# An encoder's feed-forward: every gate/up chunk by seven products, two of them run ahead

## The chip, the core and the metric

The kernel runs on one NeuronCore of a Trainium2 chip. TensorE multiplies, ScalarE and VectorE do elementwise work, GpSimd (POOL) a few small things, and DMA queues issued from SyncE (SP), ScalarE and POOL move data. The metric is the device time of one execution in microseconds (us); the time of a kernel is the median of its runs.

## The reference

Two layers over 512 tokens of width 1024, all in float32. Each layer has an attention and a convolution part with an output projection, and then a gated feed-forward:

```python
h = rms_norm(x, pre_ffn_norm[l])
g, u = jnp.split(jnp.einsum('bsd,df->bsf', h, w_gate_up[l]), 2, axis=-1)
f = jnp.einsum('bsf,fd->bsd', jax.nn.silu(g) * u, w_down[l])
x = x + rms_norm(f, post_ffn_norm[l])
```

FFN is 2816, that is 22 chunks of 128 hidden channels. Nothing else of the reference is touched by the change.

## The kernel before

**Precision.** A float32 product is made of three matmuls in a reduced format: each operand is split in a high part (a cast on ScalarE, `wh`, `big`) and a low part (a subtraction on VectorE, `wl`, `big`), and hi·hi, hi·lo and lo·hi are summed in PSUM. Weights come as `raw` tiles of 512 KB (three buffers), two for a gate/up chunk, and are split before use. `hT` are the normed tokens, turned by TensorE so that width lies on the partitions, split, in two halves of the width (g) with 512 tokens each; `raw` tiles of the same name in `out_proj` hold the turned tokens unsplit.

**An ordinary chunk** (`pair_part`) multiplies 8 slices of the width, gate and up, three matmuls each: 48 matmuls of 512 columns.

**A chunk by seven products** (`seven`) is Winograd's form of Strassen's method. The 2x2 block product of weights (width halves by gate/up) and tokens (width halves by token halves) takes seven products of 12 matmuls of 256 columns. `prepare` forms the weight differences t1 to t4 on VectorE and splits them; `make_sums` forms the four token sums once per layer, from all tokens. Products b11 and b21 give the gate for the first 256 tokens and need no sums and only the first half of the tokens; t4 gives the gate of the second half; t1, t2, t3 and b22 use the sums. Two banks y, used in turn, and banks x and q collect them.

**Order.** Chunks 0 to 3 are ordinary; 0 and 1 are done first for tokens 0 to 255 while token tiles 2 and 3 are still being normed in `out_proj`, and `turning` lets TensorE turn tile 2 inside chunk 0 and tile 3 inside chunk 1. The second halves of 0 and 1, then 2 and 3, cover `make_sums` and the first `prepare`. Chunks 4 to 21 go by seven products. TensorE's and SP's orders are those of the program text (`manual_schedule`); ScalarE's and VectorE's rows are ordered by the scheduler from the same text. Each engine has a list of its own and waits on semaphores for the others. Then the down projection splits each chunk's activation (`split`) and multiplies by the down weights.

**In `seven`, what stands between a product and the next one into the same bank** (lines 818 to 836):

```python
product(x, ops["b11"], hA[0:2], 0, 0, True)
nc.scalar.copy(y[:, :HS], x[:, :HS])
product(q, ops["t1"], sums, 1, 1, True)
product(y, ops["t2"], sums, 0, 0, False)
product(x, ops["b21"], hA, 1, 0, False)
nc.scalar.activation(gate[:, :HS], x[:, :HS], AF.Silu)
```

In ScalarE's list a row ACT_TABLE_LOAD stands where the program goes from the Ln and Exp of the norms (`rsqrt_mean`) to Silu, and where it goes back; in each layer of the kernel before that is once ahead of the first Silu and once, by `log_table`, behind the last.

## Time and profile before

| | |
|---|---|
| time, median of 3 runs | 1183.0 us (1182.74 to 1183.59) |
| the profiled execution | 1181.35 us, of it 1179.6 us span |
| TensorE (PE) busy | 1161.3 us, 98% |
| VectorE (DVE) busy | 788.5 us, 67% |
| ScalarE (ACT) busy | 628.4 us, 53% |
| granted TensorE clock | 0.998 |
| weight DMAs (`raw`), 512 KB | 192, 3.7 us from issue to landing |
| ACT_TABLE_LOAD | 6, 1283 ns each |

Matmuls overlap, so the start of one to the start of the next says how fast they go, not the duration that stands in a row. In the same way rows of VectorE and ScalarE overlap their successors by about 0.1 us. In lists of instructions a row ends with the idle time before it and who ended that, in brackets. L811 is the matmul in `product`, L190 to L192 the three of `mm3`, L241 the turning, L246 the low part of the turned tokens, L234 a norm, L761 and L762 the weight splits of `prepare`.

### The profile page before, as it was taken

To read this page: it belongs to the slowest core of one execution; us is meant where nothing else is said; L and a number is where in the kernel's file an instruction comes from. 1 tells how busy PE (TensorE), PEld (TensorE's weight loads), DVE (VectorE), ACT (ScalarE), POOL (GpSimd) and SP (SyncE) were. 2 spreads that over 40 slices of the span, in tenths; PEclk is the share of its full clock that TensorE was granted. 3 is DMA by queue.
4 is the path that set the end of the run, shared out by engine and by line. 5 is a ranking of instruction groups with operands and counts; after the bars stand their busy time and mean duration, and the time that the engine had idled before them with its cause. 6 is when DMAs were issued, how large, how long until landed. Compare 5 with 4: busy or idle time off the path is not lost.

```text
span 1179.6 us, 17833 instructions
## 1 busy us (share of the span) xinstructions
PE 1161.3 (98%) x7000; PEld 1018.9 (86%) x7000; DVE 788.5 (67%) x1330; ACT 628.4 (53%) x1217; POOL 33.8 (3%) x55
## 2 busy tenths in 40 slices
PE   9999999989999999999999999999999999999997
PEld 7777778888999999888877777788899999998886
DVE  4798655786888888432557986458868888883323
ACT  7577544663565557331445775437636555582311
POOL 5000001000000000000000000100000000000000
PEclk9999999999999999999999999999999999999999
DMA  8221123123333333423132211322223333333221
GB/s 320 90 72 54 55 66 112 56 98 99 107 99 103 106 107 110 158 74 114 46 117 80 72 54 57 99 95 72 79 90 103 106 108 108 108 126 123 91 72 72
DMA packets 33205, 114.38 MB, mean 97 GB/s; under 512 B 3936, under 2 KB 3936, under 8 KB 33120
## 3 DMA queue, kind: packets, MB, share of 16 engines
q1 hardware_dynamic: 32400, 112.15, 29.1%
q8 instruction: 55, 0.90, 0.3%
q10 hardware_dynamic: 720, 1.09, 0.2%
q14 instruction: 30, 0.25, 0.1%
HBM read 111.12 MB, written 2.10 MB: 96 GB/s over the span
## 4 chain that ended last, share of the span: by engine, by line
PE 92%; DVE 4%; ACT 2%; issue 1%; DMA 0%; DVEq 0%; SPq 0%
PE acc L811 18%; PE att L811 13%; PE acc L190 13%; PE acc L192 13%; PE acc L191 13%; PE att L190 4%; PE att L192 4%; PE att L191 4%; PE pv L427 3%; PE att L420 2%; PE att L403 1%; PE att L404 1%; ACT mid L232 1%; PE pv L192 1%; PE pv L190 1%
## 5 line engine op out<-in xcount | busy, mean ns | idle before, releaser
L178 DVE TENSOR_TENSOR wl<-raw,wh 128x1024 fp32r<-128x1024 f32 x120 | 146.5, 1222 | 165.5 <-ACT wh L177 164.9
L177 ACT CAST wh<-raw 128x1024 fp32r<-128x1024 f32 x120 | 125.7, 1050 | 177.7 <-PE acc L192 67.4
L811 PE MATMUL acc<-big,wh 128*128 128x256 f32 x1152 | 212.0, 283 | 0.0
L190 PE MATMUL acc<-big,wh 128*128 128x512 f32 (+1 forms) x496 | 184.8, 372 | 0.0
L191 PE MATMUL acc<-big,wh 128*128 128x512 f32 (+1 forms) x496 | 180.1, 363 | 1.1 <-DVE big L246 1.1
L192 PE MATMUL acc<-big,wl 128*128 128x512 f32 (+1 forms) x496 | 180.1, 363 | 0.0
L811 PEld LDWEIGHTS acc<-big,wh 128*128 128x128 f32 x1152 | 179.8, 192 | 0.2
L811 PE MATMUL acc<-big,wl 128*128 128x256 f32 x576 | 163.0, 283 | 0.0
L811 PE MATMUL att<-big,wh 128*128 128x256 f32 x864 | 160.4, 283 | 0.0
L811 PEld LDWEIGHTS att<-big,wh 128*128 128x128 f32 x864 | 134.7, 192 | 0.2
L811 PE MATMUL att<-big,wl 128*128 128x256 f32 x432 | 122.3, 283 | 0.0
L762 DVE TENSOR_TENSOR wl<-t,wh 128x1024 fp32r<-128x1024 f32 x72 | 88.0, 1223 | 43.0 <-ACT wh L761 43.0
L761 ACT CAST wh<-t 128x512 fp32r<-128x512 f32 x144 | 88.7, 619 | 45.9 <-PE att L811 31.7
L811 PEld LDWEIGHTS acc<-big,wl 128*128 128x128 f32 x576 | 110.6, 192 | 0.0
L192 PEld LDWEIGHTS acc<-big,wl 128*128 128x128 f32 x496 | 93.6, 189 | 15.2
L190 PE MATMUL acc<-wh,big 128*128 128x512 f32 x272 | 106.4, 391 | 0.2 <-ACT wh L524 0.2
L191 PEld LDWEIGHTS acc<-big,wh 128*128 128x128 f32 x496 | 93.8, 189 | 14.5 <-DVE big L246 1.7
L191 PE MATMUL acc<-wl,big 128*128 128x512 f32 x272 | 106.1, 390 | 0.2 <-DVE wl L525 0.2
L192 PE MATMUL acc<-wh,big 128*128 128x512 f32 x272 | 105.9, 389 | 0.0
L190 PEld LDWEIGHTS acc<-big,wh 128*128 128x128 f32 x496 | 93.7, 189 | 13.7 <-issue 0.8
L190 PE MATMUL att<-wh,big 128*128 128x512 f32 x228 | 89.4, 392 | 0.0
L761 ACT CAST wh<-raw 128x512 fp32r<-128x512 f32 x108 | 63.4, 619 | 48.5 <-PE acc L811 31.3
(212 smaller groups left out, 1942.9 us busy)
## 6 DMA issues: line engine op xcount, KB each, us to landing
raw<-in_w SPq DMA_DIRECT2D x192, 512.0 KB, 3.7
gain<-in_rows SPq DMA_DIRECT2D x7, 512.0 KB, 5.6
big<-in_xT SPq DMA_DIRECT2D x8, 256.0 KB, 5.5
raw<-in_w SPq DMA_DIRECT2D x8, 256.0 KB, 5.5
x<-in_x SPq DMA_DIRECT2D x4, 512.0 KB, 7.0
out_dram<-x SPq DMA_DIRECT2D x4, 256.0 KB, 2.1
out_dram<-x ACTq DMA_DIRECT2D x4, 256.0 KB, 2.1
mask_sb<-in_mask SPq DMA_DIRECT2D x1, 448.0 KB, 7.7
```

The source lines that it names most:

```text
L177: nc.scalar.copy(hi, raws[i])
L178: nc.vector.tensor_sub(lo, raws[i], hi.bitcast(F32))
L190: nc.tensor.matmul(o, sh, mh, start=start, stop=False)
L191: nc.tensor.matmul(o, sh, ml, start=False, stop=False)
L192: nc.tensor.matmul(o, sl, mh, start=False, stop=stop)
L232: nc.scalar.activation(h[:, c], x_sb[t][:, c], AF.Square, accum_out=ss[:, f:f + 1])
L403: nc.tensor.matmul(sc, qk[:, hd, q0:q0 + P], qk[:, 2 + hd, :], start=True, stop=False)
L420: nc.tensor.transpose(tp[:, k * P:(k + 1) * P], sm[:, k * P:(k + 1) * P], ident)
L427: nc.tensor.matmul(o[hd * 64:hd * 64 + 64, half * 256:half * 256 + 256], V[:, k, hc:hc + 64], PT[hd][:, k, :], start=k == 0, stop=k == NT - 1)
L761: nc.scalar.copy(hi[:, c:c + 512], src[:, c:c + 512])
L762: nc.vector.tensor_sub(lo[:, :n], src[:, :n], hi[:, :n].bitcast(F32))
L811: nc.tensor.matmul(o[:, :HS], sh[:, c], mh[:, k, :], start=start and k == 0 and n == 0, stop=k == 3 and n == 2, skip_group_check=True)
```

## The change

All 22 chunks go by seven products. The seven are cut in two functions. `lead(m)` does b11 and b21, into one bank x: b11's result is copied to the second half of the chunk's place in SBUF (`unsplit`), then b21 is added and Silu of the sum goes to the first half. `rest(m)` fetches b11's result from there into y and does t1, t2, t3 and b22; t4 (`last_product`) of a chunk is done inside the next chunk's `rest`. Six leads go ahead of all rests; tile 2 is turned behind lead 0 and tile 3 behind lead 4, each followed by its half of `make_sums`. The other 16 leads are spread over the 21 rests that have a next one, so six chunks have a rest alone. A lead loads the columns it needs of its weights by itself (two DMAs of 256 KB), and `rest` loads the whole 1 MB again. From lead 6 on its weights take the place of x in SBUF; x is written to DRAM by POOL's queue after the residual and read back behind the last chunk. Activations wait unsplit in free tiles of several kinds (`unsplit`), and the first four are split during the last chunk.

The diff, cut to its core (`load_rest` loads a `raw` half once; `quarter` takes a column range now):

```diff
-NDIRECT = 2
-
-SEVEN = 4
+LEAD = 6
+
+TURN_LEAD = {0: 2, 4: 3}
...
-    x_sb = [cpool.tile([P, D], F32, tag=f"x{t}", name=f"x{t}") for t in range(NT)]
+    x_sb = [sb.tile([P, D], F32, tag="x", bufs=4, name=f"x{t}") for t in range(NT)]
+    dpool = ctx.enter_context(tc.tile_pool(name="dpool", bufs=1, space=bass.MemoryType.DRAM))
+    x_away = dpool.tile([P, NT, D], F32, tag="x_away", name="x_away")
...
+    def load_lead(l, m):
+        if (l, m) in lead_raws:
+            return
+        if m < LEAD:
+            r = sb.tile([P, 1024], F32, tag="raw", bufs=RAW_AHEAD + 1, name=nm("raw"))
+        else:
+            r = sb.tile([P, D], F32, tag="x", bufs=4, name=nm("raw"))
+        lead_raws[l, m] = r
+        for k in range(2):
+            nc.sync.dma_start(r[:, k * 512:k * 512 + 512], w[l * NCHUNK + 16 + m][:, k * 1024:k * 1024 + 512])
+
+    def split_lead(l, m):
+        if (l, m) not in leads:
+            leads[l, m] = split_pair(lead_raws[l, m], 1024, ("wh", "wl") if m < LEAD else ("x", "x"))
+
+    def split_pair(src, n=1024, tags=("wh", "wl")):
+        hi, lo = (sb.tile([P, 1024], F32R, tag=t, bufs=4, name=nm(t)) for t in tags)
+        for c in range(0, n, 512):
+            nc.scalar.copy(hi[:, c:c + 512], src[:, c:c + 512])
+        nc.vector.tensor_sub(lo[:, :n], src[:, :n], hi[:, :n].bitcast(F32))
+        return [(hi[:, c:c + 512], lo[:, c:c + 512]) for c in range(0, n, 512)]
...
             hs[t] = normed(t, gffn)
+            nc.gpsimd.dma_start(x_away[:, t, :], x_sb[t])
...
+        def make_sums(j):
+
+            part = [[quarter(raw, g, f, j * P, P) for f in range(2)] for g in range(2)]
...
         def prepare(m):
...
+                load_rest(m, k)
+            (b11, b12), (b21, b22) = ((raws[i + k][:, :512], raws[i + k][:, 512:]) for k in range(2))
...
+            load_rest(m + 1, 1)
+            nc.vector.tensor_sub(t34[:, 512:], b21, t12[:, 512:])
             ops["t1"], ops["t2"] = split_pair(t12)
             yield
             ops["t3"], ops["t4"] = split_pair(t34)
             yield
+            ops["b22"], = split_pair(b22, 512)
+            yield
...
+        def lead(m):
+            x = bank("acc")
+            place = unsplit(m)
+            b11, b21 = leads[l, m]
+            product(x, b11, hT, 0, 0, True)
+            nc.scalar.copy(place[:, HS:], x[:, :HS])
+            product(x, b21, hT, 1, 0, False)
+            nc.scalar.activation(place[:, :HS], x[:, :HS], AF.Silu)
+
+        def last_product(m, y, up):
+            place = unsplit(m)
+            product(y, made.pop(m)["t4"], hT, 1, 1, False)
+            nc.scalar.activation(place[:, HS:], y[:, :HS], AF.Silu)
+            nc.vector.tensor_mul(place, up, place)
+
+        def rest(m, y, before, ahead):
...
+            nc.scalar.copy(y[:, :HS], unsplit(m)[:, HS:])
+            product(q, ops["t1"], sums, 1, 1, True)
+            nc.scalar.copy(p5, q[:, :HS])
+            next(ahead)
+            product(y, ops["t2"], sums, 0, 0, False)
+            nc.scalar.copy(up[:, :HS], y[:, :HS])
+            next(ahead)
+            if before is not None:
+                last_product(*before)
+            next(ahead)
+            product(y, ops["t3"], sums, 0, 1, False)
+            nc.scalar.copy(up[:, HS:], y[:, :HS])
+            nc.vector.tensor_add(up[:, HS:], up[:, HS:], p5)
+            product(q, ops["b22"], sums, 1, 0, False)
+            nc.vector.tensor_add(up[:, :HS], q[:, :HS], up[:, :HS])
+            next(ahead)
+            return m, y, up
...
+        for m in range(LEAD):
+            for k in range(m, min(m + 3, LEAD)):
+                load_lead(l, k)
+                split_lead(l, k)
+            if m + 3 < LEAD:
+                load_lead(l, m + 3)
+            lead(m)
+            if m in TURN_LEAD:
+                t = TURN_LEAD[m]
+                transposed(t, hs[t], hT, "att", raw)
+                make_sums(t - 2)
+            if m == LEAD - 3:
+                ahead = prepare(0)
+            if ahead is not None:
+                next(ahead)
+        next(ahead)
...
+        led = LEAD
+        load_lead(l, led)
+        before = None
+        for m in range(MT):
+            if led < MT:
+                split_lead(l, led)
+            before = rest(m, ys[m % 2], before, prepare(m + 1) if m + 1 < MT else down_splits())
+            if led < LEAD + (m + 1) * (MT - LEAD) // (MT - 1) and led < MT:
+                lead(led)
+                led += 1
+                if led < MT:
+                    load_lead(l, led)
+        last_product(*before)
+        for t in range(NT):
+            x_sb[t] = sb.tile([P, D], F32, tag="x", bufs=4, name=nm("x"))
+            nc.gpsimd.dma_start(x_sb[t], x_away[:, t, :])
```

**On TensorE, between b11 and b21.** `acc` and `att` are banks, `big` token tiles, `wh`/`wl` split weights. Before, in the first seven-product chunk, the last two matmuls of t2 and the first of b21:

```order
L811 MATMUL att_2779<-big_2575,wh_2730 128x256
L811 MATMUL att_2779<-big_2574,wl_2731 128x256
L811 MATMUL acc_2783<-big_2045,wh_2748 128x256
L811 MATMUL acc_2783<-big_2047,wh_2748 128x256
L811 MATMUL acc_2783<-big_2045,wl_2749 128x256 [waits DVE_49]
```

Now, in lead 0, the last two of b11 and the first of b21:

```order
L818 MATMUL acc_2370<-big_2049,wh_2288 128x256
L818 MATMUL acc_2370<-big_2047,wl_2289 128x256
L818 MATMUL acc_2370<-big_2048,wh_2288 128x256 [waits Activation_49]
L818 MATMUL acc_2370<-big_2050,wh_2288 128x256 [waits DVE_49]
L818 MATMUL acc_2370<-big_2048,wl_2289 128x256
```

b21 now follows b11 at once in the same bank and waits for ScalarE's copy of it (L829); t1 and t2 no longer stand between.

**On ScalarE, where the norms of the last tokens meet the first Silu.** Before, the first Silu (L722) stands behind all Ln and Exp rows (L208, L210) of `out_proj`; the turned tokens (L245, L248) come first:

```order
L248 COPY big_2049<-att_2412 128x4x128 [waits DVE_49]
L210 ACTIVATE small_2343<-small_2343 128x1 [waits Activation_49]
L245 CAST big_2044<-att_2468 128x4x128 [waits PE_49]
L245 CAST big_2045<-att_2476 128x4x128 [waits PE_49]
L248 COPY big_2048<-att_2468 128x4x128 [waits DVE_49]
L248 COPY big_2049<-att_2476 128x4x128 [waits DVE_49]
L752 CAST big_2521<-big_2049 128x4x256 [waits DVE_49]
L177 CAST wh_2558<-raw_2356 128x1024 [waits DMAHW1_49,PE_49]
L722 ACT_TABLE_LOAD
L722 ACTIVATE tmp_2550<-acc_2352 128x512 [waits PE_49]
```

Now the Silu of lead 0 (L831) stands among the Ln (L253) and Exp (L255) of token tile 3, and the copy of lead 1 (L829) behind them:

```order
L831 ACT_TABLE_LOAD
L831 ACTIVATE big_2371<-acc_2370 128x256 [waits PE_49]
L253 ACT_TABLE_LOAD
L253 ACTIVATE small_2336<-small_1841,small_2043 128x1
L290 CAST big_2047<-att_2398 128x4x128 [waits PE_49]
L255 ACT_TABLE_LOAD
L255 ACTIVATE small_2336<-small_2336 128x1 [waits Activation_49]
L290 CAST big_2048<-att_2406 128x4x128 [waits PE_49]
L829 COPY big_2371<-acc_2438 128x256 [waits PE_49]
```

Silu, Ln and Exp have a table load each, and the same three come once more behind the squares of tile 3, then a seventh load: seven per layer where one stood.

**On VectorE, ahead of the first rest.** `t` are weight differences, `x` a lead's split weights, L774 and L780 are `make_sums`. Before, the sums stand between ordinary chunks' work (L715, L694), ahead of the first `prepare` (L778):

```order
L754 TENSOR_TENSOR big_2522<-big_2049,big_2521 128x4x256 [waits Activation_49]
L694 TENSOR_TENSOR big_2553<-tmp_2550,big_2553 128x512 [waits Activation_49]
L754 TENSOR_TENSOR big_2575<-big_2048,big_2574 128x4x256 [waits Activation_49]
L715 TENSOR_TENSOR tmp_2622<-acc_2355,tmp_2622 128x512 [waits PE_49,Activation_49]
L754 TENSOR_TENSOR big_2575<-big_2048,big_2574 128x4x256
L178 TENSOR_TENSOR wl_2632<-raw_2556,wh_2631 128x1024 [waits DMAHW3_49,Activation_49]
L694 TENSOR_TENSOR big_2553<-tmp_2622,big_2553 128x512 [waits Activation_49]
L178 TENSOR_TENSOR wl_2664<-raw_2590,wh_2663 128x1024 [waits DMAHW4_49]
L778 TENSOR_TENSOR t_2705<-raw_2629 128x512 [waits DMAHW5_49]
```

Now the second half of the sums stands behind both chunks' `prepare` rows and lead 6's split:

```order
L800 TENSOR_TENSOR t_2673<-raw_2599,t_2673 128x512 [waits DMAHW4_49,DVE_49]
L802 TENSOR_TENSOR t_2674<-raw_2599,raw_2538 128x512 [waits DVE_49]
L222 TENSOR_TENSOR x_2652<-raw_2648,x_2651 128x1024 [waits DMAHW5_49,DMAHW6_49,DMASW2_49,Activation_49]
L222 TENSOR_TENSOR wl_2641<-raw_2534,wh_2640 128x512 [waits PE_49,Activation_49]
L291 TENSOR_TENSOR big_2049<-att_2570,big_2047 128x4x128 [waits Activation_49]
L291 TENSOR_TENSOR big_2050<-att_2578,big_2048 128x4x128 [waits Activation_49]
L804 TENSOR_TENSOR t_2674<-raw_2599,t_2673 128x512 [waits DVE_49]
L774 TENSOR_TENSOR big_2052<-big_2051,big_2052 128x4x128 [waits Activation_49]
L774 TENSOR_TENSOR big_2051<-big_2051 128x4x128 [waits DVE_49]
L774 TENSOR_TENSOR big_2051<-big_2052,big_2051 128x4x128 [waits DVE_49]
L780 TENSOR_TENSOR big_2416<-big_2052,big_2415 128x4x128 [waits Activation_49]
```

The last row is the low part that t1 of the first `rest` reads.

More of the change, by code (lines that the diff above doesn't have):

```diff
@@ L791, in prepare @@
             yield
-        def down_splits():
-            for k in (0, None, 1, None, 2, None):
-                if k is not None:
-                    split_half(2 * (l * NCHUNK + 38) + k)
-                yield
-        def seven(m, y, ahead):
-            ops = made.pop(m)
-            x, q = bank("acc"), bank("acc")
-            def product(o, weights, tiles, g, f, start):
-                hi, lo = weights
-                a, b = quarter(tiles[0], g, f), quarter(tiles[1], g, f)
-                for k in range(4):
-                    c = slice(k * P, k * P + P)
-                    for n, (sh, mh) in enumerate(((hi, a), (hi, b), (lo, a))):
-                        nc.tensor.matmul(o[:, :HS], sh[:, c], mh[:, k, :], start=start and k == 0 and n == 0,
-                                         stop=k == 3 and n == 2, skip_group_check=True)
-            hA = [[hT[k][g] for g in range(2)] for k in range(2)]
+            ops["b22"], = split_pair(b22, 512)
@@ new lines, in prepare, with product @@
+            yield
+        def product(o, weights, tiles, g, f, start):
+            hi, lo = weights
+            a, b = quarter(tiles[0], g, f), quarter(tiles[1], g, f)
+            for k in range(4):
+                c = slice(k * P, k * P + P)
+                for n, (sh, mh) in enumerate(((hi, a), (hi, b), (lo, a))):
+                    nc.tensor.matmul(o[:, :HS], sh[:, c], mh[:, k, :], start=start and k == 0 and n == 0,
+                                     stop=k == 3 and n == 2, skip_group_check=True)
@@ L815, in seven @@
+        def rest(m, y, before, ahead):
+            ops = made[m]
+            q = bank("acc")
             up = tmp([P, S])
-            gate = tmp([P, S])
             p5 = row([P, HS])
-            product(x, ops["b11"], hA[0:2], 0, 0, True)
-            nc.scalar.copy(y[:, :HS], x[:, :HS])
-            next(ahead)
+            nc.scalar.copy(y[:, :HS], unsplit(m)[:, HS:])
             product(q, ops["t1"], sums, 1, 1, True)
@@ L826, in seven @@
             next(ahead)
-            product(x, ops["b21"], hA, 1, 0, False)
-            nc.scalar.activation(gate[:, :HS], x[:, :HS], AF.Silu)
+            if before is not None:
+                last_product(*before)
             next(ahead)
@@ L887, in feed_forward @@
         hs = [None] * NT
-        done = set()
+        done = set(range(4))
         def down(f, m, t, acc, keep=None):
-            if m >= NDIRECT and m not in done:
-                split(m, unsplit(m))
+            if m not in done:
+                split(m)
             done.add(m)
@@ L913, in feed_forward @@
                     for k in range(m, min(m + 4, MT)):
[L914 to L915 removed]
+                        if k not in done:
+                            split(k)
                             done.add(k)
[L917 removed]
+                    if m == 18 - 3:
                         gpost = load_row(l, 3)
```

147 lines of the change are left out of this document (49 added, 98 removed).

## The prediction

> **What bounds the kernel now.** First the page's busy rows, then the waits of TensorE, then the chain of waits, then two stretches of layer 0: the ordinary gate/up chunks with their lead-in, and the chunks by seven products.
>
> ```profile
> span 1179.6 us, 17833 instructions
> PE 1161.3 (98%) x7000; PEld 1018.9 (86%) x7000; DVE 788.5 (67%) x1330; ACT 628.4 (53%) x1217; POOL 33.8 (3%) x55
> ...
> PE att L241 <- DVE small L213: 5.7, 2, 2.8
> ...
> PE acc L191 <- DVE big L246: 1.1, 2, 0.5
> ...
> 287.29 2.87 PE acc L811 x24
> 290.17 1.44 PE att L811 x12
> 291.61 1.44 PE acc L811 x12
> 293.05 1.44 PE att L811 x12
> 294.49 1.44 PE acc L811 x12
> 295.93 1.44 PE att L811 x12
> 297.37 2.88 PE acc L811 x24
> ...
> 236.28:287.29 51.01, 47.62 (x309) 43.33 (x308) 38.52 (x58) 27.02 (x50) 0.00 (x0) 1.00 0.31 103
> 287.29:468.88 181.59, 181.59 (x1514) 181.49 (x1513) 146.09 (x198) 110.37 (x239) 0.00 (x0) 1.00 0.33 105
> ```
>
> TensorE is the bound, at full granted clock. In 181.59 us of seven-product chunks it never stops: one chunk starts at 287.29 and the next at 297.37, 10.08 us for 84 matmuls at 0.12. In the 51 us before them it stops twice, 0.5 and 2.8 us, once each per layer, because VectorE is not ready. So a change gains only by giving TensorE less to do, and loses whatever makes TensorE wait.
>
> **What is removed: four ordinary chunks per layer.** The pace of an ordinary chunk is in these rows (start, duration, of single matmuls).
>
> ```profile
> 232.54 0.39 PE L191 MATMUL att<-wl,big 128*128 128x512 f32 x1
> 232.77 0.39 PE L192 MATMUL att<-wh,big 128*128 128x512 f32 x1
> ...
> 241.16 0.28 PE L191 MATMUL acc<-big,wh 128*128 128x256 f32 x1
> 241.28 0.28 PE L192 MATMUL acc<-big,wl 128*128 128x256 f32 x1
> 244.40 1.06 PE L241 MATMUL att<-ident,mid 128*128 128x128 f32 x8 [2.85 <-DVE small L213]
> 245.22 0.36 PE L190 MATMUL acc<-big,wh 128*128 128x256 f32 x1
> ```
>
> A 512-column matmul is issued every 0.227 us, a 256-column one every 0.12. Two full chunks are 2 x 48 x 0.227 = 21.8, two done by halves 2 x 96 x 0.12 = 23.0, together 44.8. By seven products they are 4 x 10.08 = 40.3. **Term A: -4.5 us per layer.** No more than that is on offer, plus the 3.4 us of present stalls.
>
> **What is added to every chunk: a copy with nothing over it.** In the new `lead`, b11 and b21 go one after the other into the same bank, and between them ScalarE must copy b11's result away (it is needed alone); b21's first matmul waits for that copy. Before, t1 and t2 stood between them. Rows for the cost:
>
> ```profile
> 290.20 0.37 ACT L822 COPY row<-acc 128x256 f32<-128x256 f32 x1 [0.62 <-PE acc L811]
> ...
> 236.36 0.69 DVE L246 TENSOR_TENSOR big<-acc,big 128x512 fp32r<-128x512 f32 x1
> ...
> 237.10 0.38 PE L191 MATMUL acc<-big,wh 128*128 128x256 f32 x1 [0.54 <-DVE big L246]
> 237.32 0.28 PE L192 MATMUL acc<-big,wl 128*128 128x256 f32 x1
> ```
>
> A copy starts 0.03 after the next product begins (290.17 to 290.20), lasts 0.37; an engine's end frees TensorE 0.05 later (237.05 to 237.10); the first matmul after a stop holds the next one 0.1 longer (0.22 instead of 0.12). Sum 0.55 us. Nobody else is ready on TensorE's queue: rest products stand behind b21. Bounds: 0.37 if the latencies overlap, 0.8 if ScalarE is in the middle of a cast (0.62 long, see below). I take 0.55, since the rows ahead of the copy on ScalarE have 1.44 us of b11 to finish in. Sixteen leads per layer run among the rests: **term B: +8.8 us per layer** (5.9 to 12.8). The other copies of `rest` each have one 1.44 us product over them. [...]
>
> **What is compressed: the lead-in.** Before, 46 us of ordinary chunks covered the turning of tokens 2 and 3, `make_sums` and the first `prepare`. Now six leads, 17.3 us, must cover them. TensorE's own work from 236.28 to the first rest is 17.3 + two turns of 0.82 + two dummies of 0.23 = 19.4, so without a wait the first rest would start at 255.7. It needs the sums of all tokens, which are at the end of VectorE's queue. VectorE's prices:
>
> ```profile
> 242.98 1.28 DVE L234 SCALAR_TENSOR_TENSOR mid<-x,small,gain 128x1024 f32<-128x1024 f32 x1
> ...
> 256.66 1.22 DVE L754 TENSOR_TENSOR big<-big,big 128x1024 fp32r<-128x1024 f32 x1
> 257.80 1.22 DVE L178 TENSOR_TENSOR wl<-raw,wh 128x1024 fp32r<-128x1024 f32 x1
> ...
> 270.54 0.69 DVE L778 TENSOR_TENSOR t<-raw 128x512 f32<-128x512 f32 x1
> 271.15 0.68 DVE L762 TENSOR_TENSOR wl<-raw,wh 128x512 fp32r<-128x512 f32 x1
> ```
>
> Starts are 1.14 apart for 1024 wide and 0.61 for 512. Token tile 2 is normed at 242.98 before; in the new order its Ln stands on ScalarE behind the cast of the fourth lead weight and a copy of lead 0, and I put its end at 245.0 (244.2 before). Behind it up to the lo of the last-made sum that t1 reads stand 25 operations of 512 (15.3), 5 of 1024 (5.7), two residual halves (1.3), one norm (1.2), eight small ones (1.0): 24.5 us. So VectorE alone, never waiting, lets t1 go at 269.5: **a stall of at least 13.8**.
>
> It does wait, on ScalarE and on DMA. ScalarE's new row has Silu, Ln, Exp in turn, and a table load before each:
>
> ```profile
> 469.22 0.38 ACT L837 ACTIVATE tmp<-att 128x256 f32<-128x256 f32 x1
> 469.62 1.28 ACT L221 ACT_TABLE_LOAD   x1
> 470.92 1.05 ACT L177 CAST wh<-raw 128x1024 fp32r<-128x1024 f32 x1
> ...
> L761 ACT CAST wh<-t 128x512 fp32r<-128x512 f32 x144 | 88.7, 619 | 45.9 <-PE att L811 31.7 <-ACT wh L761 12.0 <-DVE t L786 1.3
> L411 ACT ACTIVATION_READ_ACCUMULATOR row<-row,small 128x1 f32 x64 | 12.0, 187 | 0.0
> ...
> raw<-in_w SPq DMA_DIRECT2D x192, 512.0 KB, 3.7
> ```
>
> A load takes 1.3 from start to next start; seven replace one, all ahead of copies that TensorE waits for. The walk, on the axis of before: lead 0 waits for its copy (behind tile 2's squares) until 241.8, ends 243.2; turn 2 at 245.1 to 245.9; lead 1's copy stands behind a Silu load, a Ln load, a cast, an Exp load: 249.2, so b21 ends 251.1; lead 2's copy stands behind tile 3's squares, three more loads and four casts, and its Exp feeds VectorE, which meanwhile waits 3.7 us twice for a raw buffer that its own last split has just freed (246.7 and 257.2): copy 259.4, end 261.2; lead 3 ends 265.1 behind the seventh load, lead 4 268.4, turn 3 269.2, lead 5 272.6, dummies 273.0. VectorE, having waited for a third such buffer at 266.6, gives t1's lo at 275.7 instead of 269.5; the first rest's t3 waits for its own copy (no earlier last product covers it). Its four products end at 282.2 where without a wait they would end at 255.7 + 5.8 = 261.5: stalls of 20.7. Those of before, 3.4, go. **Term C: +17.3 us per layer** (10.4 by VectorE alone; 24.5 if the four loads that VectorE waits for land in 5.5 instead of 3.7, as the 256 KB loads of the first microseconds do).
>
> ```profile
> raw<-in_w SPq DMA_DIRECT2D x8, 256.0 KB, 5.5
> ```
>
> [...]
>
> **At nothing.** Steady VectorE per chunk: four differences, b22's lo and the gate 6 x 0.61, two splits 2.28, two short adds some 0.7, a lead split 1.14: 7.8 of the 10.6 us that TensorE takes (6.6 of 7.2 in the six chunks without a lead); ScalarE seven casts at 0.52 and eight short rows at about 0.28, 5.9. The b11/b21 weights are read twice, 1.5 MB per chunk or 145 GB/s, where slice 1 of the page moved 320. x goes to DRAM and back on POOL's queue, 4 MB per layer, needed again only at the residual, behind the whole first half of the down projection (264 matmuls at 0.227, 60 us). If this cover failed, it is rival 3.
>
> ```profile
> GB/s 320 90 72 54 55 66 112 56 98 99 107 99 103 106 107 110 158 74 114 46 117 80 72 54 57 99 95 72 79 90 103 106 108 108 108 126 123 91 72 72
> ```
>
> **Sum.** -4.5 + 8.8 + 17.3 = +21.6 per layer, +43.2 for two. The profiled execution took 1181.35 (span 1179.6), 1.65 under the median: 1224.6 for a profile, **1226 us** against the median of 1183.0.
>
> **Rivals.**
> 1. It does what arithmetic says: the copies slip under weight loads and ScalarE reaches its rows earlier, so both layers keep A and lose the 3.4 us of stalls: 1183.0 - 2 x 7.9 = 1167. For it: sevens run without a gap now. Against: an in-order TensorE and an explicit wait in every lead; VectorE's 24.5 us against 10.7 of cover. To be faster at all it needs B and C together under 4.5, a sixth of the 26.1 I have. Faster: 0.06.
> 2. Only the lead-in costs: the copy is hidden (e.g. the wait costs under 0.15): 1183.0 + 2 x (-4.5 + 2.4 + 17.3) = 1213; with VectorE's bound for C, 1200. 0.12.
> 3. The rest stage itself becomes bound by VectorE or ScalarE, since each waits in order for TensorE's products and for raws freed late; one more microsecond on 21 chunks: 1226 + 42 = 1268. For it: VectorE busy 146 of 182 now. Against: chunk m+1's operands are made one whole chunk ahead. 0.08.
> [...]
>
> **How the numbers follow.** My forecast has 0.66, the rivals 0.06, 0.12, 0.08, 0.04, and 0.04 is left for cases between that net to nothing. A measurement here can tell 0.2%, 2.4 us. Slower: 0.66 + 0.12 + 0.08 + 0.04 = 0.90; same 0.03; faster 0.07. Range: low ends of B and C, 2 x (-4.5 + 5.9 + 10.4) = +23.6, 1207, taken to 1202 since rival 2 reaches 1200; high ends 2 x (-4.5 + 12.8 + 24.5) = +66, 1249, taken to 1247.
>
> **What would show it.** Right: in the waits of TensorE a row "acc <- ACT" of the L829 copy, some 40 times and near 0.4 to 0.5 us, plus a few of several us; fourteen table loads on ScalarE at L831, L253 and L255, where two stood at L722; two to three waits of 2 to 8 us per layer between the out-projection and the first rest; rest chunks with a lead 10.6 us apart, without one 7.2. Wrong: rests spaced more than 10.9 (rival 3), leads of 2.9 us without a gap (rivals 1 and 2), or the first rest starting under 20 us after the out-projection.

## The result, and the profile after

The changed kernel takes **1259.0 us** (median of four runs, 1252.66 to 1263.58) against 1183.0: 1.064 times the time before, 95% interval 1.059 to 1.069. The forecast was 1226, 1202 to 1247: the sign was right, the size was not.

The page's busy rows, and then TensorE's waits (us in total, times, longest), answer to the rows shown of before, where TensorE was busy 98% of the span and waited for nobody among the sevens:

```profile
span 1250.9 us, 18425 instructions
...
PE 1175.6 (94%) x7096; PEld 1030.5 (82%) x7096; DVE 821.5 (66%) x1410; ACT 679.3 (54%) x1361; POOL 43.5 (3%) x71
```

```profile
PE acc L818 <- ACT big L829: 41.0, 24, 7.5
PE acc L818 <- ACT mid L829: 7.1, 8, 2.1
PE acc L818 <- ACT gain L829: 6.7, 8, 1.9
...
PE acc L818 <- ACT u L829: 1.8, 4, 0.5
```

These are the 44 leads of both layers, each waiting for its own copy (L829). Before, gate/up of layer 0 lasted from 236.28 to 468.88, 232.6 us. Now it is 50.2 us up to the end of the first rest's four products, and 217.6 more to the start of the last matmul (columns: stretch, its length, busy time of PE, PEld, DVE, ACT, POOL, granted clock, DMA share, GB/s):

```profile
236.21:286.40 50.19, 31.94 (x211) 29.33 (x210) 40.14 (x67) 38.71 (x77) 1.06 (x2) 0.86 0.37 126
286.40:504.00 217.60, 202.96 (x1659) 199.66 (x1658) 160.14 (x228) 123.89 (x279) 2.15 (x4) 1.00 0.46 148
```

To the end of that matmul, at 504.23, it is 268.0, 35.4 more than before in layer 0; layer 1 has 268.3, 35.7 more. Together that is 71.1 of the 71.3 us between the two profiled executions (1252.66 and 1181.35), so nothing outside gate/up matters.

**The lead-in.** TensorE's waits in order of time:

```profile
241.59 0.80 PE L818 MATMUL acc<-big,wh 128*128 128x256 f32 x2 [3.00 <-ACT big L829]
...
251.03 0.50 PE L818 MATMUL acc<-big,wh 128*128 128x256 f32 x2 [3.48 <-ACT big L829]
262.34 0.80 PE L818 MATMUL acc<-big,wh 128*128 128x256 f32 x2 [6.68 <-ACT big L829]
267.73 0.51 PE L818 MATMUL acc<-big,wh 128*128 128x256 f32 x2 [0.97 <-ACT big L829]
```

And ScalarE's list between the first two copies, where a table is loaded three times for one Silu, one Ln and one Exp:

```profile
244.97 1.28 ACT L831 ACT_TABLE_LOAD   x1
246.27 0.38 ACT L831 ACTIVATE big<-acc 128x256 f32<-128x256 f32 x1
246.66 1.28 ACT L253 ACT_TABLE_LOAD   x1
247.95 0.29 ACT L253 ACTIVATE small<-small,small 128x1 f32<-128x1 f32 x1
...
248.74 1.28 ACT L255 ACT_TABLE_LOAD   x1
250.03 0.20 ACT L255 ACTIVATE small<-small 128x1 f32<-128x1 f32 x1
...
250.60 0.38 ACT L829 COPY big<-acc 128x256 f32<-128x256 f32 x1
```

The stops stand where the walk had them, but the long ones are followed by matmuls at half the granted clock (the last column but two):

```profile
242.00:244.00 2.00, 2.00 (x11) 2.00 (x11) 1.93 (x6) 0.47 (x3) 0.00 (x0) 0.50 0.67 212
252.00:254.00 2.00, 2.00 (x11) 2.00 (x11) 1.68 (x3) 1.17 (x3) 0.53 (x1) 0.50 0.00 0
262.00:264.00 2.00, 1.66 (x7) 1.66 (x8) 2.00 (x3) 0.81 (x3) 0.00 (x0) 0.50 0.03 8
```

**The rests.** Two leads, one with a copy in time and one with a late one:

```profile
304.61 1.60 PE L818 MATMUL acc<-big,x 128*128 128x256 f32 x12
306.24 0.37 ACT L829 COPY big<-acc 128x256 f32<-128x256 f32 x1 [0.42 <-PE acc L818]
306.67 1.70 PE L818 MATMUL acc<-big,x 128*128 128x256 f32 x12 [0.46 <-ACT big L829]
308.21 0.40 PE L818 MATMUL acc<-big,wh 128*128 128x256 f32 x2
...
334.31 1.60 PE L818 MATMUL acc<-big,x 128*128 128x256 f32 x12
...
336.49 0.62 ACT L221 CAST x<-raw 128x512 fp32r<-128x512 f32 x1 [2.99 <-DMA raw<-in_w]
...
337.53 0.61 ACT L221 CAST x<-raw 128x512 fp32r<-128x512 f32 x1
338.05 0.36 ACT L829 COPY big<-acc 128x256 f32<-128x256 f32 x1
338.47 1.69 PE L818 MATMUL acc<-big,x 128*128 128x256 f32 x12 [2.56 <-ACT big L829]
```

Twelve matmuls at 0.12 would let b21 follow at 306.05; it starts at 306.67, and what comes behind it 0.10 late: 0.72 us for a copy in time. The second copy stands on ScalarE's list behind casts of the *next* lead's weights (`x`), and the first of these waits 2.99 us for its DMA. In layer 0 the 16 waits add up to 14.6 us, of which eight are 0.46. The DMA was late: it stood on SP's queue behind two loads that wait for a raw buffer. Its median time to landing is also longer than that of a load of 512 KB; whether that comes from its size or from its place is tested below (SP's list, and the DMA issues with size and median time to landing):

```profile
328.57 1.53 SPq L115 DMA_DIRECT2D raw<-in_w  x2
330.15 0.90 SPq L212 DMA_DIRECT2D raw<-in_w  x2
```

```profile
raw<-in_w SPq DMA_DIRECT2D x192, 512.0 KB, 3.9
raw<-in_w SPq DMA_DIRECT2D x96, 256.0 KB, 5.2
```

### The profile page after: what moved, and what is told of

Same layout as the page of the kernel before. It is cut to its first block, busy times and chain, and to the rows that moved or that the text cites. A ratio compares the mean times of both kernels' runs of the same rounds, so it can differ in the third digit from the quotient of the medians.

```text
span 1250.9 us, 18425 instructions
## 1 busy us (share of the span) xinstructions
PE 1175.6 (94%) x7096; PEld 1030.5 (82%) x7096; DVE 821.5 (66%) x1410; ACT 679.3 (54%) x1361; POOL 43.5 (3%) x71
## 4 chain that ended last, share of the span: by engine, by line
PE 79%; ACT 9%; DMA 7%; DVE 4%; issue 2%; DVEq 0%; SPq 0%; ACTq 0%
PE acc L818 16%; PE att L818 11%; PE acc L235 10%; PE acc L237 10%; PE acc L236 10%; DMA raw<-in_w 7%; PE att L235 4%; PE att L237 4%; PE att L236 4%; PE pv L472 3%; PE att L465 2%; ACT wh L221 2%; PE att L448 1%; PE att L449 1%; ACT x L221 1%
## 5 line engine op out<-in xcount | busy, mean ns | idle before, releaser
L818 PE MATMUL acc<-big,wh 128*128 128x256 f32 x896 | 176.4, 295 | 31.0 <-ACT big L829 25.5
L818 PE MATMUL att<-big,wh 128*128 128x256 f32 x1056 | 192.7, 284 | 1.7 <-ACT tmp L851 1.7
L818 PEld LDWEIGHTS acc<-big,wh 128*128 128x128 f32 x896 | 146.8, 201 | 35.6 <-ACT big L829 27.3
L221 ACT CAST wh<-t 128x512 fp32r<-128x512 f32 x176 | 107.7, 618 | 48.0 <-PE att L818 38.9
L818 PE MATMUL acc<-big,x 128*128 128x256 f32 x768 | 105.8, 288 | 29.3 <-ACT big L829 15.6
L818 PEld LDWEIGHTS acc<-big,x 128*128 128x128 f32 x768 | 96.3, 192 | 35.8 <-ACT big L829 18.8
L235 PE MATMUL acc<-big,wh 128*128 128x512 f32 x304 | 123.4, 406 | 0.0
L237 PE MATMUL acc<-big,wl 128*128 128x512 f32 x304 | 119.2, 392 | 0.0
L236 PE MATMUL acc<-big,wh 128*128 128x512 f32 x304 | 118.8, 391 | 0.0
L818 PEld LDWEIGHTS att<-big,wl 128*128 128x128 f32 x528 | 101.5, 192 | 0.0
L818 PEld LDWEIGHTS acc<-big,wl 128*128 128x128 f32 x448 | 90.3, 201 | 0.0
L235 PE MATMUL att<-wh,big 128*128 128x512 f32 x228 | 89.4, 392 | 0.0
L237 PE MATMUL att<-wh,big 128*128 128x512 f32 x228 | 88.9, 390 | 0.0
```

What stands on the lines that cost most here:

```text
L221: nc.scalar.copy(hi[:, c:c + 512], src[:, c:c + 512])
L235: nc.tensor.matmul(o, sh, mh, start=start, stop=False)
L236: nc.tensor.matmul(o, sh, ml, start=False, stop=False)
L237: nc.tensor.matmul(o, sl, mh, start=False, stop=stop)
L818: nc.tensor.matmul(o[:, :HS], sh[:, c], mh[:, k, :], start=start and k == 0 and n == 0, stop=k == 3 and n == 2, skip_group_check=True)
```

## The experiments

All times are medians of four runs; changes are against 1259.0 unless another kernel is named. "Lead-in" below is from the first product of a layer to the two dummy matmuls ahead of the first rest, "rests" from there to the last product, in the profile, layer 0 and layer 1. The changed kernel has 41.1 and 39.9, and 226.9 and 228.4.

### The exposed copy, covered

```diff
+            if led is not None:
+                x = lead_first(led)       # b11 and its copy
             product(q, ops["b22"], sums, 1, 0, False)
...
+            if led is not None:
+                lead_second(led, x)       # b21 and Silu
```

> Edit: for the 16 leads that go among the rests, b11 and the copy of its result are put ahead of b22 of the rest that they follow, and b21 behind b22, so that the copy has one product of 1.44 us over it. Theory A (the exposed copy is the loss of the rest stage): in the changed kernel each of these copies holds TensorE for 0.46 to 2.56 us by the waits, 14.6 us per layer, and with the 0.16 that the last matmul drains and the 0.10 of a restart 18.9 us per layer (217.6 us from 286.4 to 504.0 against 198.7 of matmuls at 0.12). With 1.44 us of cover the nine at 0.46 vanish and the late ones shrink to under 1 us: 14 to 18 us less per layer, 1259 - 28 to 36 = 1223 to 1231. Theory B (ScalarE, VectorE or late weights bound the rest stage, rival 3): the stop only moves to t1 or t2 of the next rest, and the time falls by less than 10, to no better than 1249.

1231.7 us (1227.2 to 1233.2), **27.3 less**, just outside theory A's range and far from theory B's; between the profiled executions it is 19.6. The rests are 216.5 and 216.1, 10.4 and 12.3 shorter; the lead-ins, 41.8 both, are 0.7 and 1.9 longer. So theory A holds: the loss of this stage is mostly the exposed copy, not VectorE's or ScalarE's rate, both of which did the same work in less time. A few late copies still show through the product that covers them, and two of them, of 1.77 us, started the half clock. First the row of one in TensorE's list (12 matmuls in 2.29 us instead of 1.70), then the stretch behind it:

```profile
376.35 2.29 PE L818 MATMUL acc<-big,x 128*128 128x256 f32 x12 [1.77 <-ACT big L836]
```

```profile
378.00:380.00 2.00, 2.00 (x11) 2.00 (x11) 1.60 (x3) 0.38 (x1) 0.00 (x0) 0.50 0.67 186
```

### Late weights

```diff
-                split_lead(l, led)
+                split_lead(l, led, raws[2 * (base + m + 1)])   # and no load_lead from lead 6 on
```

> Edit: the leads among the rests don't load weights of their own; their casts read the raw tile of the next chunk, which is there already, so the gates of chunks 6 to 21 are computed from other weights. Left out: 32 DMAs of 256 KB per kernel and layer. Theory A1 (the seven or so copies per layer that come later than 0.46 are late because ScalarE's list has the next lead's casts ahead of them, and these wait for a 256 KB load that lands after 5.2 us, 32.3 us of waiting in all): all 16 waits fall to 0.46, 7.3 us less per layer, 1259 - 15 = 1244. Theory A2 (ScalarE's or VectorE's own work makes them late): the late ones stay, and the time is within 4 us of 1259.

1239.5 us (1238.5 to 1240.6), **19.5 less**; the rests are 219.8 and 220.0, 7.1 and 8.4 shorter. With no load to wait for the late copies are gone (the 24 `big` waits of both layers fall from 41.0 to 34.0 us, the 8 `mid` ones from 7.1 to 4.5): A1 rather than A2. This kernel has less traffic too, so the next one keeps the data and moves only the place on the queue:

```diff
                 split_lead(l, led)
+                if led + 1 < MT:
+                    load_lead(l, led + 1)   # instead of behind lead(led)
```

> Edit, of the changed kernel alone: in the loop of the rests the two DMAs of the next lead's weights stand on SP's queue ahead of the loads of the next rest instead of behind them (and one rest earlier where a rest has no lead). Same data, same casts. Theory A1 (a lead's copy is late where its successor's weights were queued on SP behind two loads that wait for a raw buffer: at 328.57 these wait until a difference on VectorE frees one, the lead's load goes out at 330.15, and the cast that stands ahead of the copy waits for it 2.99 us): the waits over 0.46 go, 7 us per layer as in e2_noload, 1259 - 14 to 20 = 1239 to 1245. Rival (the 256 KB loads land late by themselves, 5.2 us, and e2_noload gained by less traffic, 114 instead of 144 GB/s): at most half of it, not below 1250.

1251.3 us (1248.6 to 1253.3), **7.7 less**: half of what theory A1 expected, and inside the rival's range. But the rival's reason falls. All copies in the rests but the last are at 0.46 now, and the 256 KB loads land in 3.9 us (median) instead of 5.2, with the same data: their place on the queue had made them late, not their size. Part of the stop moved to t3 of the rests, which waits for the copy of t2's result (L851), as in

```profile
327.31 0.50 PE L818 MATMUL att<-big,wh 128*128 128x256 f32 x2 [0.72 <-ACT tmp L851]
```

Four such in layer 0 and five in layer 1 cost 2.8 and 2.3 us, drain and restart included, beside the first rest's own. The rests, 226.3 and 225.5, are only 0.6 and 2.9 shorter in this profile, though the copies give back 7. In layer 0 TensorE stands 4.4 us less but is busy 3.8 more (213.9 us against 210.1): some 1.5 of it is a stretch at half clock (0.50 in 282 to 284) and some 1.3 the drains of eight more waits. The lead-in of layer 1, which the edit doesn't touch, is 3.6 longer. So the queue's place is the cause of the late copies, but in a kernel with this many stops half of what they cost is lost again. e1_cover with the same edit (g0_cover_load, below) gains 3.9, with ranges that overlap, and e7_cover_silu 6.0.

### The table loads

```diff
-            nc.scalar.activation(place[:, :HS], x[:, :HS], AF.Silu)
+            nc.scalar.copy(place[:, :HS], x[:, :HS])      # leads 0 to 3
...
+        for m in range(4):                                # behind the last lead of the lead-in
+            tc.keep_in_program_order(nc.scalar.activation(unsplit(m)[:, :HS], unsplit(m)[:, :HS], AF.Silu))
```

> Edit: the sums of leads 0 to 3 are copied out as they are, and their Silu is done in place behind the norm of token tile 3, so that ScalarE loads its table once per layer in the lead-in instead of seven times; four more short rows. Theory (the lead-in is longer than its 19.4 us of matmuls because the leads' copies queue on ScalarE behind six more table loads of 1.28 us, beside VectorE): the first rest's four products end 6 to 9 us earlier than 50.2 us after the start of gate/up, 1259 - 12 to 18 = 1241 to 1247. Rival (VectorE's 24.5 us behind the norm of tile 2 and the raw buffers set the end, the loads only fill waits): under 3 us per layer, not below 1253.

1247.5 us (1243.7 to 1248.4), **11.5 less**, just short of the 12 to 18 expected. The table is loaded once per layer ahead of the rests instead of seven times. The lead-in of the changed kernel, and then of this one, up to the dummies:

```profile
236.21:277.33 41.12, 25.04 (x161) 23.26 (x160) 31.23 (x54) 32.45 (x63) 1.06 (x2) 0.83 0.43 143
```

```profile
236.37:267.57 31.20, 23.69 (x161) 21.89 (x160) 28.13 (x51) 23.69 (x57) 1.06 (x2) 0.89 0.57 185
```

9.9 us less here, and 8.3 in layer 1; 3.9 and 5.4 come back in the rests (230.8, 233.8), where the first sums are now waited for and the first leads' copies are later. With the copy covered as well, less of that comes back:

> Edit: both, the b11 of the 16 leads ahead of b22 (as in e1_cover, which took 27.3 us off 1259.0) and the Silu of leads 0 to 3 behind the norm of tile 3 (as in e3_silu, 11.5 off). Theory A (the two losses stand in different stages and don't share a cause): they add, 1259.0 - 38.8 = 1220, between 1215 and 1225. Rival (what is saved in the lead-in comes back as late weights in the rests, of which e3_silu's profile shows 4 to 5 us per layer: rest stage 230.8 and 233.8 us against 226.9 and 228.4): the cover hides these too, and the sum is better than added, under 1215.

1214.6 us (1213.8 to 1216.1), 44.4 less, so better than the sum of the two, and by 0.4 us in the rival's range. In the profile the rests are 2.3 and 1.4 us longer than e1_cover's, instead of 3.9 and 5.4: the cover hides part of what came back, as the rival has it. Against e1_cover the table loads are worth 17.1 us.

### The half clock

```diff
             nc.scalar.copy(place[:, HS:], x[:, :HS])
+            for n in range({0: 20, 1: 20, 2: 40}.get(m, 0)):
+                nc.tensor.matmul(warm[:, :HS], hT[0][0][:, 0, :P], hT[0][0][:, 0, :HS], start=n == 0, stop=True, ...)
             product(x, b21, hT, 1, 0, False)
```

> Edit: in leads 0, 1 and 2, between b11 and b21, 20, 20 and 40 matmuls of 256 columns whose result nobody reads are put on TensorE's list, 2.4, 2.4 and 4.8 us at full clock, which is under or near the stops that stand there (3.0, 3.5 and 6.7 us in layer 0). Theory C (the stops lower the granted clock, to 0.50 in 242 to 244, 252 to 254 and 262 to 264, and the matmuls behind them at 0.21 instead of 0.12 cost 4 us per layer, since a lead's Silu and with it ScalarE's list begin later): the clock of the lead-in stays near 1.0 and the time falls by 5 to 9 us, to 1250 to 1254. Rival (slow matmuls there only fill what would be a stop anyway, or the clock falls for another reason): no fall, 1257 to 1262, or up to 4 us more where the added matmuls outlast a stop (lead 1 of layer 1 stops for only 0.5). [...]

1258.1 us (1254.6 to 1260.8): **no gain**, though the lead-ins are 38.2 and 38.9 us, 2.9 and 1.1 shorter. The rests of this execution lost it again: 235.3 and 230.6 us, 8.4 and 2.2 longer; in layer 0 seven waits for a copy are over 0.9 us instead of five, and the mean clock is 0.97. While the rests have stops of their own this doesn't tell whether theory C fails, so the next pair has the copies covered and the loads first.

> Edit: e1_cover with the lead's load first on SP's queue; the lead-in stays that of the changed kernel, with its stops of 3, 3 and 6.5 us and its half clock. It is the base of g1_cover_load_warm, with hardly a stop left in the rests. As f1_cover_silu_load stands to e7_cover_silu, 6.0 us under e1_cover: 1224 to 1228.

> Edit: g0_cover_load with the 20, 20 and 40 unread matmuls between b11 and b21 of leads 0, 1 and 2, as in e4_warm. Theory C (the half clock behind the lead-in's stops delays the leads' Silus and with them all of ScalarE's list; e4_warm's profile had the first rest 2.9 and 1.1 us earlier, and only the rests, with half clock behind their own stops, took it back): without stops in the rests the gain shows in the time, 4 to 7 us less than g0_cover_load. Rival (the matmuls that nobody reads cost elsewhere what they save in the lead-in, or the lead-in's end is VectorE's): within 2 us of g0_cover_load.

1227.8 (1226.0 to 1231.1) without the unread matmuls and **1221.7** (1220.4 to 1223.2) with them: 6.1 us less for 80 more matmuls per layer. Lead-ins without, then with them:

```profile
236.41:276.39 39.98, 24.35 (x161) 22.47 (x160) 30.84 (x53) 32.45 (x64) 1.06 (x2) 0.83 0.49 161
842.67:884.67 42.00, 27.39 (x162) 25.50 (x160) 30.74 (x53) 32.48 (x64) 1.06 (x2) 0.76 0.45 154
```

```profile
236.54:275.72 39.18, 30.56 (x242) 28.91 (x240) 30.83 (x54) 32.77 (x64) 1.06 (x2) 1.00 0.51 161
840.44:879.46 39.02, 30.52 (x242) 28.89 (x241) 30.85 (x54) 32.74 (x64) 1.06 (x2) 1.00 0.48 162
```

The clock goes from 0.83 and 0.76 to 1.00, and the lead-ins are 0.8 and 3.0 us shorter; the rests, 214.3 and 215.4 without, are 212.9 and 212.8 with them. So theory C holds, some 3 us per layer; of it 0.8 and 3.0 stand in the lead-ins.

### VectorE, and more leads ahead

> Edit: as e3_silu, and the weights of the first six leads have no low part (the high part is used in its place), so VectorE has 6 x 1.14 = 6.8 us less to do in the lead-in and TensorE the same number of matmuls; left out: the low parts of these weights. Theory V (with the table loads gone VectorE's list alone sets the end of the lead-in): from the start of gate/up to the first rest's sums 5 to 7 us less per layer than e3_silu's 31.2 and 31.6, 1247.5 - 10 to 14 = 1234 to 1238. Rival S (ScalarE's casts and copies, 23.7 of 31.2 busy, or the raw buffers set it): under 3 us per layer, not below 1242.

1239.2 us (1232.2 to 1241.9), 8.4 under e3_silu, for 13.6 us of VectorE work left out: between theory V's range and the rival's. The lead-ins are 27.2 and 29.1, 4.0 and 2.5 shorter where theory V has 5 to 7. VectorE is a limit there once the table loads are gone, but not the only one. The cure by more leads first failed:

```diff
-LEAD = 6
+LEAD = 10                     # and the places of chunks 6 to 9 and 14 to 17 change sides
```

> Edit: as e7_cover_silu, and ten leads ahead of all rests instead of six (the places of chunks 6 to 9 and 14 to 17 change sides, so that no tile is waited for). Theory V (what is left of the lead-in is VectorE's list, busy 28.1 of 31.2 us in e3_silu, and it is cured by more TensorE work ahead that brings VectorE little): four leads more give TensorE 11.5 us and VectorE 4.6, so the stops of the lead-in fall by some 7 us per layer against e7_cover_silu, and four fewer leads stand among the rests; gate/up takes 237 to 242 us per layer instead of some 252, and the kernel 1192 to 1202. Rival R (the leads are bound by their raw buffers and DMAs, 512 KB each 2.9 us, with three raw buffers): the leads ahead come no faster than one in 4 us, and the time stays within 5 us of e7_cover_silu's.

1220.9 us (1218.1 to 1223.4), 6.4 *more* than e7_cover_silu. VectorE has time now, but each lead pays its exposed copy, some 3.6 us from one to the next:

```profile
253.00 0.50 PE L818 MATMUL acc<-big,wh 128*128 128x256 f32 x2 [0.46 <-ACT big L829]
256.62 0.50 PE L818 MATMUL acc<-big,wh 128*128 128x256 f32 x2 [0.48 <-ACT big L829]
```

> Edit: e7_cover_silu with the lead's load first on SP's queue. Theory A1: what is left over matmuls in the rests of e7_cover_silu (218.8 and 217.5 us against 204.5) is the first rest's 5 us and late weights under the cover; with the latter gone 2 to 5 us less per layer, 1214.6 - 4 to 10 = 1205 to 1211. Rival: no change, 1212 to 1217.

1208.6 us (1206.7 to 1209.6), 6.0 under e7_cover_silu, as theory A1 has it.

```diff
-            lead(m, m < 4)
+            x = lead_first(0) if m == 0 else x_next
+            if m + 1 < LEAD:
+                x_next = lead_first(m + 1)          # b11 of the next lead covers this one's copy
+            lead_second(m, x, m < 4)
```

> Edit: e6_lead10 with the lead's load first on SP's queue, and in the lead-in b11 of lead m+1 ahead of b21 of lead m, so that these ten copies too have a product over them. Theory E (e6_lead10 came out no faster than e7_cover_silu because each lead in the lead-in pays the exposed copy, 3.60 us from one to the next instead of 2.88, so four more of them give VectorE time but cost as much): lead-in 45.3 - 7 = 38 to 40, rests 204 - 5 = 199, together 237 to 240 us per layer, 1192 to 1199. Rival (leads are bound by ScalarE, 34.5 of 45.3 busy, or by their loads): lead-in stays above 43, 1210 or above.

> Edit: f2_pipe10 with eight leads ahead instead of ten. Theory V (what VectorE still has to do is covered by ten leads and not quite by eight): stops of 2 to 4 us more per layer ahead of the first rest, two leads more among the rests at no cost, so 2 to 6 us slower than f2_pipe10. Rival (the end of the lead-in is VectorE's and does not depend on the leads): the same as f2_pipe10 within 2 us, or faster, since each lead ahead costs VectorE 1.14 us.

**1201.7** us with ten leads ahead (1201.1 to 1202.4) and **1201.5** with eight (1200.4 to 1202.3): 19.2 under e6_lead10, of which some 6 are the load's place by f1_cover_silu_load. Theory E holds in direction: the lead-ins are 42.3 and 40.4 us instead of 45.3 and 45.4, but not the 38 to 40 that were expected, and the time misses the 1192 to 1199. Ten and eight leads make no difference in the time, as the rival of f3_pipe8 has it, but not for its reason: with eight the lead-ins end 8.5 and 7.0 us earlier, and stops of 3.75 and 2.31 us, of the size that theory V had, stand in the first rest. What is left over matmuls in f2_pipe10 is 11.4 and 9.5 us of the lead-ins (30.9 of matmuls) and 5 and 11 of the rests (198.3 and 204.0, 193 of matmuls). It is still 18.6 us over the kernel before.

```diff
-        nc.vector.tensor_sub(lo[:, :n], src[:, :n], hi[:, :n].bitcast(F32))
+        sub.tensor_sub(lo[:, :n], src[:, :n], hi[:, :n].bitcast(F32))    # sub is nc.gpsimd for the leads ahead
```

> Edit: f2_pipe10 with the low parts of the ten lead weights formed on POOL instead of VectorE. Theory V (what is left of the lead-in, 42.3 and 40.4 us against 30.9 of matmuls, is VectorE's list, where two leads wait 1.45 and 1.90 for a low part that stands behind sums): VectorE loses 11.4 us, the stops for low parts go, 3 to 5 us less per layer, 1192 to 1197. Rival P (POOL's subtraction takes more than the 2.9 us of a lead, no row here shows one of this size): leads wait for POOL, and it is slower than f2_pipe10's 1201.7.

> Edit: g2_pipe10_pool with six leads ahead instead of ten. With VectorE relieved of 6.8 us, theory V has the sums 24.5 - 6.8 = 17.7 us behind the norm of tile 2, at some 263 where six leads without stops would end near 258: 2 to 5 us more of stops per layer than with ten leads, 2 to 8 us slower than g2_pipe10_pool. Rival P: fewer POOL rows ahead of the rests, so faster than g2_pipe10_pool.

1215.2 (1212.6 to 1217.1) and 1216.7 (1214.9 to 1218.4): 13.5 and 15.0 more than f2_pipe10. Rival P has the outcome, but not the cause: POOL takes 2.5 us, less than the 2.9 of a lead. Some leads do wait for it (1.41, 0.76 and 4.70 us in layer 0 of g2_pipe10_pool), but the larger loss is ahead of the first product, which begins 5.0 us later in both layers (241.43 instead of 236.41 in layer 0): 10 of the 13.5. It waits for a cast of the turned tokens, which stands on ScalarE's list behind squares that wait 3.94 us for VectorE, and VectorE's rows last until POOL has subtracted (2.33 us for one of 0.21, last section); in f2_pipe10 the scheduler has that cast ahead of the squares. That fewer POOL rows are faster, the second half of rival P, doesn't show.

### One ordinary chunk less

```diff
-SEVEN = 4
+SEVEN = 3
```

> Edit, of the kernel before: three ordinary chunks instead of four per layer, the fourth goes by seven products; nothing else. The matmuls fall by 21.8/2 - 10.08 = 0.8 us per layer. Theory V (the ordinary chunks are the cover of VectorE's work ahead of the first sums: 38.5 us of VectorE in 51 of the lead-in; with 40 us and 35 of VectorE, sums and the first weights just about come in time): 1180 to 1184, the same as before by 0.2%. Rival (the cover was already short): stops of 2 us and more per layer ahead of the first seven products, 1187 or above.

1182.7 us, ratio 0.9984 to before's runs beside it (0.9972 to 0.9995): 0.6 to 3.3 us less, around the 1.6 that term A's arithmetic gives for one chunk per layer. No stop appears ahead of the first sevens. In the profile, gate/up of layer 1 takes 232.0 us, 0.6 less than before, but that of layer 0 takes 233.3, 0.7 more. There the turning of tile 2, behind a stop of 2.85 us, takes 1.94 us, and the matmuls behind it start 0.21 apart up to 247.23 and 0.12 from there:

```profile
244.00 1.94 PE L241 MATMUL att<-ident,mid 128*128 128x128 f32 x8 [2.85 <-DVE small L213]
```

In the kernel before the same eight matmuls take 1.06 us behind a stop of the same length (244.40). This kernel is the only one here that isn't slower than before, and by less than 0.2% in the middle.

## Why the prediction was wrong in size

The direction and the main mechanism, copies and stops that TensorE waits for, were right. Three steps failed: the price of a copy in time (term B), the late weights, which stood at nothing, and the full clock behind the stops of the lead-in (term C).

**What bounds the kernel, term A.** Right. The pace of 0.12 held in rests and leads (2.88 for 24 matmuls at full clock), and the small dose of A in e8_before_seven3 came out near what was computed, where the clock stayed full.

**Term B, 8.8 us per layer: mis-sized, 18.8 measured in layer 0** (14.6 of waits, and 0.26 of drain and restart for each of the 16). Two steps failed. The first is a misread row. The copy was priced to start 0.03 us after the next product begins, at 290.17 in the chain of waits. But that chain begins a piece where the one before it ends; in the list of instructions the same product of the kernel before begins at 290.00:

```profile
290.00 0.40 PE L811 MATMUL att<-big,wh 128*128 128x256 f32 x2
```

So that copy (290.20) starts 0.20 after the moment at which the next product can begin, and the copies of the changed kernel start 0.19 after it (306.05 to 306.24): the last matmul must first have ended, 0.16 later. A copy in time costs 0.72 and not 0.55: 2.7 us per layer. The second step is the late copies, 7.3 us per layer, which were not in the sum: it was said that "the rows ahead of the copy on ScalarE have 1.44 us of b11 to finish in", without asking whether one of them waits for a DMA. The bound of 0.8 per copy was set by one cast, not by a transfer.

**Term C, 17.3 us: right in its walk, low by 4.3 and 3.2.** Turn 2 and the stops of leads 0, 1 and 2 came within 3 us of their forecast times, and the first rest's four products end 50.2 us after the start instead of 45.9. The walk let all matmuls run at 0.12 behind stops of 3 to 7 us. In layer 0 the stretches at half clock lose 1.2, 1.5 and 1.2 us (from start to start, 12 matmuls behind 241.59 take 2.7 instead of 1.5, 24 behind 251.03 4.5 instead of 3.0, 12 behind 262.34 2.7), and each delays the lead's Silu and all that follows on ScalarE. By this arithmetic the clock makes 3.9 of the 4.3. The experiments give back less: with the unread matmuls the lead-ins are 2.9 and 1.1 us shorter (e4_warm) and 0.8 and 3.0 (g1_cover_load_warm), so what makes the rest of the miss stays open. The profile of before shows no half clock in gate/up: its longest stop there is 2.85 us, at a granted clock of 1.00.

**At nothing.** VectorE's and ScalarE's rates were covered, as said, and x on POOL's queue cost nothing that shows. The weights read twice were not free: f5_load_first, which reads as much, has no late copies, so not by their bandwidth (148 GB/s in the rests) but by their place on SP's queue and on ScalarE's list.

**From the profile to the median.** The profiled execution, 1252.66, is 28.1 over the forecast for it. That is the two layers at some 14. Another 4.7 come from the median lying 6.3 over the profiled execution, where 1.65 was carried over from before: the four runs have mean granted clocks of 0.985, 0.984, 0.981 and 0.977 in the order of their times. Which stops lost the clock in the slower runs isn't seen, since they have no trace; that e2_noload and f2_pipe10, without late copies, spread by 2 us and the changed kernel by 11 speaks for the stops in the rests, but f5_load_first, without them too, spreads by 4.7.

**Signs and rivals.** The signs named are there: 44 waits for the copy, 14 table loads (6 at L831, 4 each at L253 and L255), three long stops in layer 0 (3.00, 3.48 and 6.68 us) and two in layer 1 (2.85 and 7.52), rests with a lead 10.8 apart. Rivals 1 and 2 fell: the copies are exposed, all 44 of them. 3 has its sign (rests more than 10.9 apart) where a late copy made 11.7 of 10.8. The half of it that says "raws freed late" came true, through SP's queue, at 7.3 us per layer instead of 21; that the rate of VectorE or ScalarE bounds the rests is refuted by e1_cover. The 0.04 of the fourth stood for a switch that costs more than its row, and no run shows that term: what stands behind a load starts 0.02 after it (246.27 behind 244.97 + 1.28). The table loads themselves, 7.7 us in six, cost 8.5 per layer.

## What to carry to other kernels

A product that must be copied out before the next one can use its bank needs another product between the two; alone it costs the drain, the copy, the semaphore and the restart, here 0.72 us each (0.19, 0.37, 0.06 and 0.10), and it makes TensorE wait for whatever ScalarE's list holds ahead of the copy, DMAs included. When work is taken out of a lead-in that covers another engine, price the stops it opens with the slow matmuls behind them (0.21 us apart instead of 0.12 here). Functions of different tables should not alternate on a list that TensorE waits for: in the lead-in here each change between Silu, Ln and Exp came with a load of 1.28 us. And when a start of an instruction enters a price, read it from the list of instructions, not from the chain of waits.

## What was not expected of the hardware

- **The half clock followed a stop of 1.77 us and not one of 2.56 us.** Behind the first, in e1_cover, the granted clock was 0.50; behind the second, in the changed kernel ahead of 338.47, it stayed at 1.00. Behind one of 2.85 us eight matmuls took 1.94 us in e8_before_seven3 and 1.06 in the kernel before. In the trace of the changed kernel, its first 5 and last 20 us left out, six stretches have a granted clock of 0.50: 241.41 to 244.82, 251.65 to 255.06, 258.48 to 265.30, 862.64 to 869.46, 876.29 to 886.53 and 1081.09 to 1084.50. They last 3.41 us or two or three times that, and all their beginnings and ends lie whole numbers of 3.413 us apart. With the trace divided into such steps, each of the six follows a step at full clock in which TensorE stands idle for 62% or more by the profile's rows; the other 341 steps at full clock are idle for 54% at most, and full clock follows them. Steps of this length at the two stops, first e1_cover, then the changed kernel:

```profile
373.75:377.16 3.41, 1.64 (x13) 1.43 (x13) 1.96 (x4) 1.76 (x4) 0.00 (x0) 1.00 0.34 82
377.16:380.57 3.41, 3.41 (x19) 3.41 (x17) 2.52 (x3) 0.56 (x2) 0.00 (x0) 0.50 0.76 237
```

```profile
333.57:336.98 3.41, 2.34 (x20) 2.13 (x18) 2.17 (x4) 0.49 (x1) 0.00 (x0) 1.00 0.52 184
336.98:340.39 3.41, 1.92 (x16) 1.93 (x17) 2.73 (x5) 1.63 (x5) 0.00 (x0) 1.00 0.25 56
```

  The stop of 1.77 us lies within one step and leaves it 52% idle. The longer one falls on two, 31% and 44% idle. A share near 50% is not decisive by these rows: in the changed kernel the steps from 995.76 and 1036.72, 50% and 54% idle, kept the full clock. The steps don't lie alike in the two traces (from 241.41, a beginning in the changed kernel, to 377.16, one in e1_cover, is 39.8 of them), so in these runs the length of a stop alone doesn't tell whether it costs the clock; what sets the steps is not shown. That this also spreads the times of a kernel with many stops is likely, but not shown. Matmuls whose result nobody reads, put into the stops of the lead-in, made a kernel 6.1 us faster (g1_cover_load_warm against g0_cover_load).
- **VectorE's rows that began while POOL subtracted lasted until POOL had done.** In g2_pipe10_pool, POOL's rows and then VectorE's in the same stretch:

```profile
245.03 2.38 POOL L223 TENSOR_TENSOR wl<-raw,wh 128x1024 fp32r<-128x1024 f32 x1 [4.01 <-ACT wh L222]
247.87 2.78 POOL L223 TENSOR_TENSOR wl<-raw,wh 128x1024 fp32r<-128x1024 f32 x1 [0.46 <-ACT wh L222]
```

```profile
245.10 2.33 DVE L259 SCALAR_TENSOR_TENSOR small<-small,small 128x1 f32<-128x1 f32 x1
...
247.66 0.75 DVE L675 SCALAR_TENSOR_TENSOR x<-tmp,small,x 128x512 f32<-128x512 f32 x1
248.32 2.89 DVE L675 SCALAR_TENSOR_TENSOR x<-row,small,x 128x512 f32<-128x512 f32 x1
```

  The operation on one column, 0.21 us in f2_pipe10 (mean of its L258), takes 2.33 and ends at 247.43, POOL's row at 247.41; the last one, 0.75 in f2_pipe10 (L674), takes 2.89 and ends 0.56 behind POOL's second row. The one from 247.66, which began before that row, takes its 0.75. With 11.4 us of VectorE's work moved to POOL the lead-ins are 46.4 and 44.8 us instead of 42.3 and 40.4.
